# The last stage of a hybrid mixing layer: gated products summed in PSUM, operand casts moved to ScalarE, the residual gate folded into the output weights

## The chip, the cores and the metric

The kernel runs on one core of a Trainium2 chip. The metric is the device time of one execution in microseconds (us), taken as the median of several runs; lower is better. The engines are PE (TensorE, the matrix unit), DVE (VectorE), ACT (ScalarE), POOL (GpSimd) and SP (SyncE, which here only issues transfers). Each engine works through its own list of instructions strictly in order; semaphores make one engine wait for another. SBUF is the working memory, PSUM the small memory (eight banks of 128 x 512 fp32) that PE writes its products to.

## The reference

One layer over 2048 positions of width 1024: a normalised and modulated input is projected, three branches (short convolution `a`, Fourier mixing `f`, neighbourhood attention `c`) give one 2048 x 512 array each, and then, in the part that matters here:

```
y_a = (...) @ w_br_a;  y_f = (...) @ w_br_f;  y_c = (...) @ w_br_c       # each 512 -> 1024
m   = sig(g_a)*y_a + sig(g_f)*y_f + sig(g_c)*y_c                         # 1024 wide
x   = x + gt_l * (m @ w_out)                                             # residual gate gt_l: one number per output column
return rmsnorm(x, final_g)
```

## The kernel before, in words

All matrix work is fp32 in three passes: each operand is split into a high part (a cast to the fp32r type) and a low part (operand minus high part), and `mm3` (lines 125 to 128) issues high x high, high x low, low x high into one PSUM bank. `split` (line 130) does the cast on one engine (line 131) and the subtraction on another (line 132).

The kernel first computes projections, attention and the Fourier part; the order of instructions on each engine is set by the scheduler of the framework, from the program's order, its dependencies and the buffers that it may use. The last stage (lines 1206 to 1273) starts while the last pair of projections is still being computed. It works on four blocks of 512 positions. For each block:

- **Branch operands** (`make_y`, line 1151). For each of the three branches and four pieces k: load the piece (`yr`, two buffers) and its partner, multiply them (line 1177, DVE), cast the product to `yh` and subtract to get `yl`, both on DVE (line 1181). The pieces of the first block are made during the last pair of projections; those of a later block are made while the output products of the block before it run.
- **Branch products** (lines 1228 to 1247). For each of eight output pieces j and three branches: load the weights (`load_wb`: cast `wbh` on ACT, subtraction `wbl` on POOL, three buffers each), load the stored gate `th` (it holds tanh(g/2), so that sig(g) is half of `th` + 1), 12 matmuls into a bank `mm` from `bank()`, which rotates through three banks. DVE then computes (`th` + 1) x bank into SBUF (line 1238) and adds the branches there (line 1240). The sum `acc` is split into `mh` (ACT) and `ml` (DVE). A matmul group of the next output piece needs a free bank: line 1238 of three groups earlier.
- **Output weights** (`load_wo`, line 1212), in the first block only: eight loads of 128 x 1024 through two buffers (`wor`), split into `woh` (ACT) and `wol` (DVE), then kept.
- **Output products** (lines 1248 to 1273). For four tiles of 128 positions and two halves x: 24 matmuls into a bank `po` (two banks), DVE multiplies the bank by the gate `gtb` (line 1261), POOL adds the residual `xr` (line 1262; DVE in the very last tile), ACT squares it and sums along the row (line 1263), then two tiny DVE operations and a POOL power (lines 1264 to 1266) give the row's scale, DVE applies it together with `fg` (line 1269), and SP stores the tile. The buffer `xr` is free for its next load once ACT has squared.

POOL's list holds the 24 `wbl` subtractions of a block, then the eight adds and four powers of its output products, then the 24 of the next block.

Of the kernel before, what the change touches and what calls it, by code (L numbers as in the profile page):

```python
# [11 lines left out]
F32 = mybir.dt.float32  # L12
F32R = mybir.dt.float32r
AF = mybir.ActivationFunctionType
ALU = mybir.AluOpType
# [44 lines left out]
def emit(tc, I, out, dbg=None):  # L60
    nc = tc.nc
# [22 lines left out]
    vtt = nc.vector.tensor_tensor  # L84
    ptt = nc.gpsimd.tensor_tensor
    stt = nc.vector.scalar_tensor_tensor
# [38 lines left out]
    def mm3(ps, ah, al, bh, bl, first, last):  # L125
        nc.tensor.matmul(ps, ah, bh, start=first, stop=False)  # L126
        nc.tensor.matmul(ps, ah, bl, start=False, stop=False)  # L127
        nc.tensor.matmul(ps, al, bh, start=False, stop=last)  # L128

    def split(hi, lo, src, heng, leng):  # L130
        heng.copy(hi, src) if heng is nc.scalar else heng.tensor_copy(hi, src)  # L131
        return leng.tensor_tensor(lo, src, hi.bitcast(F32), ALU.subtract)  # L132
# [27 lines left out]
    def then(a, b):  # L160

        tc.add_manual_dep(b.ins, a.ins.name, mybir.DependencyInfo(mybir.DependencyClass.NoSync, mybir.DependencyReason.DATA), reason="order")
# [151 lines left out]
    def bank():  # L314
        return pm.tile([128, 512], F32, tag="mm", name="mm")
# [827 lines left out]
    c2, pc, wcv, gtb = (C[x] for x in ("c2", "pc", "wcv", "gtb"))  # L1143

    def htile(o, hl, k, name):
        return hpool.tile([128, 512], F32R, tag=f"{o}{hl}{k}", name=name)
# [4 lines left out]
    def make_y(b, br, behind=None):  # L1151
        bs = slice(b * 512, b * 512 + 512)
        for k in range(4):
            yr = c2.tile([128, 512], F32, tag="yr", name="yr")
            load(yr, {"a": sad, "f": sfd, "c": scd}[br][k][b])
            o = c2.tile([128, 512], F32, tag="yo", name="yo")
            if br == "a":
                u = c2.tile([128, 514], F32, tag="u", name="u")
                lo, hi = max(b * 512 - 1, 0), min(b * 512 + 513, S)
                if b == 0:  # L1160
                    nc.vector.memset(u[:, 0:1], 0.0)
                if b == NB - 1:
                    nc.vector.memset(u[:, 513:514], 0.0)
                load(u[:, lo - b * 512 + 1 : hi - b * 512 + 1], ud[k][:, lo:hi])
                nc.scalar.activation(o, u[:, 0:512], AF.Identity, bias=wcv[:, k, 3:4], scale=wcv[:, k, 0:1])
                i = stt(o, u[:, 1:513], wcv[:, k, 1:2], o, ALU.mult, ALU.add)
                if behind:
                    then(behind, i)
                stt(o, u[:, 2:514], wcv[:, k, 2:3], o, ALU.mult, ALU.add)
            elif br == "f":  # L1170
                load(o, fd[k][:, bs])
            else:
                u = c2.tile([128, 514], F32, tag="u", name="u")
                load(u[:, :512], od[k][:, b].rearrange("p a b -> p (a b)"))
                nc.scalar.copy(o.rearrange("p (r ct c) -> p ct r c", r=8, ct=4)[:, :, ::-1, :],
                               u[:, :512].rearrange("p (ct r c) -> p ct r c", ct=4, r=8))
            i = vtt(yr, yr, o, ALU.mult)  # L1177
            if behind:
                then(behind, i)
            a, l = htile(YT[br], "h", k, "yh"), htile(YT[br], "l", k, "yl")  # L1180
            split(a, l, yr, nc.vector, nc.vector)
            yh[br, k], yl[br, k] = a, l

    def load_wb(j, n_):
        wr = c2.tile([128, 512], F32, tag="wr", name="wr", bufs=WRB)
        nc.sync.dma_start(wr, I["w_br"][j, n_])
        wh = c2.tile([128, 512], F32R, tag="wbh", name="wbh", bufs=3)
        wl = c2.tile([128, 512], F32R, tag="wbl", name="wbl", bufs=3)
        split(wh, wl, wr, nc.scalar, nc.gpsimd)
        return wh, wl  # L1190
# [4 lines left out]
    def hook():  # L1195
        br = next(first_y, None)
        if br:
            make_y(0, br)
            wb0.append(load_wb(0, len(wb0)))
# [12 lines left out]
    def load_wo(k):  # L1212
        wr = c1.tile([128, D], F32, tag="xn", name="wor", bufs=2)
        nc.sync.dma_start(wr, I["w_out"][:, k])
        for x in range(2):
            if k < 4:
                woh[k][x], wol[k][x] = (htile(("B22", "T4")[x], hl, k, "wo") for hl in "hl")
            else:
                woh[k][x], wol[k][x] = (c1.tile([128, 512], F32R, tag=f"wo{hl}{k}{x}", name="wo") for hl in "hl")
            split(woh[k][x], wol[k][x], wr[:, x * 512 : x * 512 + 512], nc.scalar, nc.vector)  # L1220

    for b in range(NB):
        bs = slice(b * 512, b * 512 + 512)
        if b:
            for br in "afc":
                make_y(b, br, done)
        mh, ml = [], []
        for j in range(8):
            acc = None
            for n_, br in enumerate("afc"):  # L1230
                wh, wl = wb0.pop(0) if wb0 else load_wb(j, n_)
                th = c2.tile([128, 512], F32, tag="tg", name="tg", bufs=4)
                nc.sync.dma_start(th, gd[n_ * 8 + j][b])
                ps = bank()
                for k in range(4):
                    s = slice(k * 128, k * 128 + 128)
                    mm3(ps, wh[:, s], wl[:, s], yh[br, k], yl[br, k], k == 0, k == 3)
                nc.vector.scalar_tensor_tensor(th, th, 1.0, ps, ALU.add, ALU.mult)  # L1238
                if acc is not None:
                    nc.vector.tensor_tensor(th, th, acc, ALU.add)  # L1240
                acc = th
            for k in (((0, 1),) + tuple((k,) for k in range(2, 8)) + ((),))[j] if b == 0 else ():
                load_wo(k)
            a, l = htile(("T1", "T3")[j // 4], "h", j % 4, "mh"), htile(("T1", "T3")[j // 4], "l", j % 4, "ml")
            done = split(a, l, acc, nc.scalar, nc.vector)
            mh.append(a)
            ml.append(l)
        for t in range(4):
            ts_ = slice(t * 128, t * 128 + 128)
            row = b * 512 + t * 128  # L1250
            end = row == S - 128
            xn = c1.tile([128, D], F32, tag="xn", name="xn", bufs=2)
            sm = c2.tile([128, 4], F32, tag="smc", name="smc")
            for x in range(2):
                cs = slice(x * 512, x * 512 + 512)
                xr = c2.tile([128, 512], F32, tag="xr", name="xr")
                load(xr, I["x"][row : row + 128, cs])
                ps = pc.tile([128, 512], F32, tag="po", name="po")
                for k in range(8):
                    mm3(ps, mh[k][:, ts_], ml[k][:, ts_], woh[k][x], wol[k][x], k == 0, k == 7)  # L1260
                vtt(xn[:, cs], ps, gtb[:, cs], ALU.mult)  # L1261
                (vtt if end else ptt)(xn[:, cs], xn[:, cs], xr, ALU.add)  # L1262
                nc.scalar.activation(xr, xn[:, cs], AF.Square, accum_out=sm[:, x : x + 1])
            nc.vector.tensor_tensor(sm[:, 2:3], sm[:, 0:1], sm[:, 1:2], ALU.add)
            nc.vector.tensor_scalar(sm[:, 2:3], sm[:, 2:3], 1.0 / D, 1e-6, ALU.mult, ALU.add)
            nc.gpsimd.tensor_tensor(sm[:, 3:4], sm[:, 2:3], mhalf[:, 0:1], ALU.pow)
            for x in range(2):
                cs = slice(x * 512, x * 512 + 512)
                nc.vector.scalar_tensor_tensor(xn[:, cs], xn[:, cs], sm[:, 3:4], fg[:, cs], ALU.mult, ALU.mult)  # L1269
                if end:  # L1270
                    (nc.sync, nc.scalar)[x].dma_start(out[row:, cs], xn[:, cs])
            if not end:
                store(out[row : row + 128, :], xn)
# [92 lines left out]
```

## Time and profile before

| | |
|---|---|
| runs (three) | median 2257.54 us, 2255.1 to 2263.36 |
| profiled execution, its own time | 2256.13 us |
| its span in the trace | 2254.4 us |
| busy in the span | PE 2132.9 us (95%), DVE 1547.0 (69%), ACT 887.1 (39%), POOL 1011.5 (45%) |
| last stage | first branch matmul 1766.69, last output matmul ends about 2246.4 |

The span is what the trace covers; the device time is 1.7 us longer. PE is busy nearly all the time, so what can be gained is the time in which PE waits, or runs at a lower clock after it waited. Two traps: matmuls are pipelined, so that a matmul's own duration (0.39 us) is longer than the 0.23 us at which they follow one another; and an engine's busy share says nothing on whether PE waits for it. The useful views are those that show, for one stretch, how long PE was not busy and which instruction ended that.

### The profile page before, as it was taken

How to read it: one execution, taken by the hardware profiler on the slowest of the kernel's cores; microseconds unless marked ns; L12 is line 12 of the kernel's file. 1: busy time of each engine (PE TensorE's matmuls, PEld its weight loads, DVE VectorE, ACT ScalarE, POOL GpSimd, SP SyncE). 2: the span in 40 equal slices, each digit the busy share in tenths (PEclk: the TensorE clock that was granted, in tenths of full speed). 3: DMA queues.
4: the chain of work that ended last, by engine and by line, in shares of the span. 5: the costliest groups of instructions: out<-in, count | busy, mean ns of one | idle time of the engine just before them, and what ended most of it. 6: DMA issues, size and time to landing. Idle time of an engine off the chain costs nothing. (4 is left out here: it accounts for less than half of the span.)

```text
span 2254.4 us, 32033 instructions
## 1 busy us (share of the span) xinstructions
PE 2132.9 (95%) x10588; PEld 1686.6 (75%) x10588; DVE 1547.0 (69%) x2731; ACT 887.1 (39%) x2011; POOL 1011.5 (45%) x761
## 2 busy tenths in 40 slices
PE   6899989999999899999999999999999898999998
PEld 4678768888788687777777777777757677878777
DVE  6864685565665665778787788786736868787773
ACT  3443222334544442454555555554213332222121
POOL 2753467654464654444444334343415243434341
PEclk8999999999999899999999999999999999999999
DMA  6244644233233344343444444453466676666561
GB/s 255 80 136 117 225 174 168 94 108 117 94 101 111 101 142 131 109 126 107 142 127 127 139 148 127 141 149 127 154 211 218 212 223 214 192 206 191 173 190 67
DMA packets 198863, 336.78 MB, mean 149 GB/s; under 512 B 22249, under 2 KB 89129, under 8 KB 197546
## 3 DMA queue, kind: packets, MB, share of 16 engines
q1 hardware_dynamic: 198554, 334.47, 46.8%
q8 instruction: 84, 1.38, 0.3%
q14 instruction: 81, 0.66, 0.1%
q10 hardware_dynamic: 144, 0.26, 0.0%
HBM read 248.27 MB, written 86.38 MB: 148 GB/s over the span
## 5 line engine op out<-in xcount | busy, mean ns | idle before, releaser
L131 ACT CAST wh<-wr 128x512 fp32r<-128x512 f32 x384 | 237.7, 620 | 479.1 <-PE mm L311 388.1
L132 DVE TENSOR_TENSOR wl<-wr,wh 128x512 fp32r<-128x512 f32 x256 | 244.7, 957 | 37.0 <-ACT wh L131 36.8
L132 POOL TENSOR_TENSOR wl<-wr,wh 128x512 fp32r<-128x512 f32 x128 | 173.7, 1360 | 212.8 <-ACT wh L131 191.0
L337 POOL TENSOR_TENSOR ws<-wr 128x512 f32<-128x512 f32 x62 | 89.0, 1435 | 309.0 <-DMA wr<-w_in 255.3
L395 DVE SCALAR_TENSOR_TENSOR st<-mm,bin,tp 128x512 f32<-128x512 f32 x158 | 118.0, 747 | 143.0 <-PE mm L312 136.0
L132 POOL TENSOR_TENSOR wbl<-wr,wbh 128x512 fp32r<-128x512 f32 x96 | 130.9, 1367 | 163.0 <-ACT wbh L131 160.4
L126 PE MATMUL mm<-yh,wbh 128*128 128x512 f32 x384 | 153.5, 400 | 17.8 <-DVE tg L1238 10.4
L128 PE MATMUL mm<-yh,wbl 128*128 128x512 f32 x384 | 152.8, 398 | 2.3 <-POOL wbl L132 2.3
L127 PE MATMUL mm<-yl,wbh 128*128 128x512 f32 x384 | 151.8, 396 | 0.3 <-DVE yl L132 0.3
L931 PE MATMUL tr<-ident,P 128*128 128x128 f32 (+3 forms) x672 | 120.4, 280 | 19.1 <-DVE PT L941 7.9
L132 POOL TENSOR_TENSOR wl<-ws,wh 128x512 fp32r<-128x512 f32 x62 | 83.7, 1350 | 112.5 <-ACT wh L131 94.8
L931 PEld LDWEIGHTS tr<-ident,P 128*128 128x128 f32 (+3 forms) x672 | 78.9, 139 | 68.4 <-DVE PT L941 25.4
L355 POOL TENSOR_TENSOR wr<-wr 128x512 f32<-128x512 f32 x64 | 87.9, 1373 | 93.7 <-DVE wl L132 58.8
L450 DVE TENSOR_TENSOR st<-mm,tp 128x512 f32<-128x512 f32 x96 | 65.9, 686 | 87.2 <-PE mm L312 84.4
L310 PE MATMUL mm<-B11h,wh 128*128 128x512 f32 x256 | 104.5, 408 | 14.0 <-DVE tp L353 7.4
L131 ACT CAST wbh<-wr 128x512 fp32r<-128x512 f32 x96 | 59.2, 620 | 127.6 <-PE mm L127 61.0
L126 PE MATMUL po<-wo,mh 128*128 128x512 f32 x256 | 101.2, 395 | 7.8 <-DVE xn L1261 7.7
L310 PE MATMUL mm<-T4h,wh 128*128 128x512 f32 x256 | 103.1, 403 | 4.5 <-DVE tp L345 4.5
L311 PE MATMUL mm<-B11l,wh 128*128 128x512 f32 x256 | 103.0, 402 | 4.2 <-DVE B11l L132 4.2
L339 POOL TENSOR_TENSOR wr<-ws,wr 128x512 f32<-128x512 f32 x62 | 84.3, 1360 | 49.6 <-DVE wl L132 36.3
L310 PE MATMUL mm<-B21h,wh 128*128 128x512 f32 x256 | 102.6, 401 | 3.6 <-DVE st L450 2.8
L310 PE MATMUL mm<-T2h,wh 128*128 128x512 f32 x256 | 102.8, 402 | 1.4 <-ACT T2h L131 1.4
(319 smaller groups left out, 6293.3 us busy)
## 6 DMA issues: line engine op xcount, KB each, us to landing
wr<-w_in SPq DMA_DIRECT2D x136, 512.0 KB
gd<-st SPq DMA_DIRECT2D x96, 256.0 KB
wr<-w_br SPq DMA_DIRECT2D x96, 256.0 KB
tg<-gd SPq DMA_DIRECT2D x96, 256.0 KB
tab<-dft SPq DMA_DIRECT2D x40, 256.0 KB
wa<-w_ada SPq DMA_DIRECT2D x32, 256.0 KB
rawq<-qd SPq DMA_DIRECT2D x64, 128.0 KB
rawk<-kd SPq DMA_DIRECT2D x64, 128.0 KB
```

The costliest lines, as they stand in the source:

```text
L126: nc.tensor.matmul(ps, ah, bh, start=first, stop=False)
L127: nc.tensor.matmul(ps, ah, bl, start=False, stop=False)
L128: nc.tensor.matmul(ps, al, bh, start=False, stop=last)
L131: heng.copy(hi, src) if heng is nc.scalar else heng.tensor_copy(hi, src)
L132: return leng.tensor_tensor(lo, src, hi.bitcast(F32), ALU.subtract)
L310: nc.tensor.matmul(ps, w[0][:, s], oh, start=first and k == 0, stop=False)
L311: nc.tensor.matmul(ps, w[0][:, s], ol, start=False, stop=False)
L337: ptt(t1, a21, a22, ALU.add)
L339: ptt(a11, t1, a11, ALU.subtract)
L355: ptt(a12, a12, a11, ALU.subtract)
L395: stt(dst, ps, bc(m), add, ALU.add, ALU.add)
L931: nc.tensor.transpose(pt[:w_, x * 128 : x * 128 + 128], src, ident)
```

## The change

Five edits, all in the last stage.

1. The cast to `yh` moves from DVE to ACT (48 casts in all; the subtraction `yl` stays on DVE and so now waits for ACT).
2. Branch products go in turn to a bank of `bank()` (three) and of a new set `pb` (three): six banks in place of three.
3. The gated product of the second and third branch is written back to its own PSUM bank and added from there: into the SBUF tile for the second, into the PSUM bank for the third. `split` then reads the sum from PSUM.
4. `load_wo` multiplies the loaded 128 x 1024 output weights by the gate (one DVE operation per load, eight in all) ahead of the split.
5. The output products are no longer multiplied by the gate; one DVE operation adds the residual to the bank. POOL's add is gone.

```diff
-            split(a, l, yr, nc.vector, nc.vector)
+            split(a, l, yr, nc.scalar, nc.vector)
...
         nc.sync.dma_start(wr, I["w_out"][:, k])
+        vtt(wr, wr, gtb, ALU.mult)
...
+    turn_ = iter(range(1 << 20))
+
+    def branch_bank():
+        return pc.tile([128, 512], F32, tag="pb", name="pb", bufs=3) if next(turn_) % 2 else bank()
...
-                ps = bank()
+                ps = branch_bank()
...
-                nc.vector.scalar_tensor_tensor(th, th, 1.0, ps, ALU.add, ALU.mult)
-                if acc is not None:
-                    nc.vector.tensor_tensor(th, th, acc, ALU.add)
-                acc = th
+                if acc is None:
+                    stt(th, th, 1.0, ps, ALU.add, ALU.mult)
+                    acc = th
+                else:
+                    stt(ps, th, 1.0, ps, ALU.add, ALU.mult)
+                    vtt(acc if n_ == 1 else ps, ps, acc, ALU.add)
...
-            done = split(a, l, acc, nc.scalar, nc.vector)
+            done = split(a, l, ps, nc.scalar, nc.vector)
...
-                vtt(xn[:, cs], ps, gtb[:, cs], ALU.mult)
-                (vtt if end else ptt)(xn[:, cs], xn[:, cs], xr, ALU.add)
+                vtt(xn[:, cs], ps, xr, ALU.add)
```

The line numbers of the changed kernel are seven higher behind `load_wo`: the add of product and residual is its line 1269, the two scalings its 1276, the gate multiplication of the weights its 1215, the two gating operations its 1245 and 1248, the branch add its 1249.

DVE's list in the output products of the first block, between the third and the fourth bank of output products, before (line 1261 empties a bank):

```order
L1261 TENSOR_TENSOR xn<-po,gtb 128x512
L1177 TENSOR_TENSOR yr<-yr,yo 128x512
L131 CAST yh<-yr 128x512
L132 TENSOR_TENSOR yl<-yr,yh 128x512
L1177 TENSOR_TENSOR yr<-yr,yo 128x512
L131 CAST yh<-yr 128x512
L132 TENSOR_TENSOR yl<-yr,yh 128x512
L1261 TENSOR_TENSOR xn<-po,gtb 128x512
```

The same place of the changed kernel (its line 1269 empties a bank):

```order
L1269 TENSOR_TENSOR xn<-po,xr 128x512
L1177 TENSOR_TENSOR yr<-yr,yo 128x512
L132 TENSOR_TENSOR yl<-yr,yh 128x512
L1177 TENSOR_TENSOR yr<-yr,yo 128x512
L132 TENSOR_TENSOR yl<-yr,yh 128x512
L1269 TENSOR_TENSOR xn<-po,xr 128x512
```

The two casts are gone from DVE's list; the multiplication (line 1177) that waits for a load still stands ahead of the next emptying.

DVE's list at the start of the stage, from the emptying of j = 0's second product on, before (the rows for `yr` and `yo` make the operands of branch `c`; the first line 1238 empties j = 0's second product, the next one j = 1's first):

```order
L1238 SCALAR_TENSOR_TENSOR tg<-tg,mm 128x512
L132 TENSOR_TENSOR yl<-yr,yh 128x512
L1240 TENSOR_TENSOR tg<-tg 128x512
L1238 SCALAR_TENSOR_TENSOR tg<-tg,mm 128x512
L1177 TENSOR_TENSOR yr<-yr,yo 128x512 x2
L131 CAST yh<-yr 128x512 x2
L132 TENSOR_TENSOR yl<-yr,yh 128x512 x2
L132 TENSOR_TENSOR wo<-wor,wo 128x512 x2
```

The same place of the changed kernel, down to the first gate multiplications of output weights:

```order
L1248 SCALAR_TENSOR_TENSOR pb<-tg,pb 128x512
L132 TENSOR_TENSOR yl<-yr,yh 128x512
L1249 TENSOR_TENSOR tg<-pb,tg 128x512
L1177 TENSOR_TENSOR yr<-yr,yo 128x512 x2
L132 TENSOR_TENSOR yl<-yr,yh 128x512
L1245 SCALAR_TENSOR_TENSOR tg<-tg,pb 128x512
L132 TENSOR_TENSOR yl<-yr,yh 128x512
L1248 SCALAR_TENSOR_TENSOR mm<-tg,mm 128x512
L1215 TENSOR_TENSOR wor<-wor,gtb 128x1024
L1249 TENSOR_TENSOR mm<-mm,tg 128x512
L1215 TENSOR_TENSOR wor<-wor,gtb 128x1024
```

The last two multiplications of branch `c` (line 1177, x2) stood behind the emptying of j = 1's first product; they now stand ahead of it, and two multiplications of 1024 columns follow.

PE's list in the first block, where the third output piece j = 2 begins (`mm_17659` is the last product of j = 1, `mm_17696` the first of j = 2), before:

```order
L126 MATMUL mm_17659<-yh_17431,wbh_17653 128x512
L127 MATMUL mm_17659<-yl_17432,wbh_17653 128x512
L128 MATMUL mm_17659<-yh_17431,wbl_17654 128x512
L126 MATMUL mm_17696<-yh_17254,wbh_17690 128x512
L127 MATMUL mm_17696<-yl_17255,wbh_17690 128x512
```

The same place of the changed kernel (`pb_17661` and `mm_17699` are those products, `po_18182` and `po_18211` the first two banks of output products, `wo_17585` and `wo_17589` the first output weights, `mh_17604` the first sum):

```order
L126 MATMUL pb_17661<-yh_17431,wbh_17655 128x512
L127 MATMUL pb_17661<-yl_17432,wbh_17655 128x512
L128 MATMUL pb_17661<-yh_17431,wbl_17656 128x512
L126 MATMUL po_18182<-wo_17585,mh_17604 128x512
L126 MATMUL po_18211<-wo_17589,mh_17604 128x512
L126 MATMUL mm_17699<-yh_17254,wbh_17693 128x512
L127 MATMUL mm_17699<-yl_17255,wbh_17693 128x512
```

Two matmuls of the output products now stand ahead of j = 2; before, the first of them stood behind all three branches of j = 2.

## Rows read from the trace of the kernel before

**Rows 1.** Windows of PE: us, busy (matmuls), granted clock, DMA share, GB/s.

```profile
1766.60:1806.20 39.60, 31.12 (x116) 0.91 0.75 245
1806.20:1849.10 42.90, 42.22 (x178) 1.00 0.73 226
1849.10:1894.70 45.60, 43.33 (x188) 1.00 0.69 222
1894.70:1912.00 17.30, 12.91 (x50) 0.90 0.56 179
...
1966.20:2013.00 46.80, 44.47 (x193) 1.00 0.66 210
2013.00:2028.40 15.40, 12.97 (x50) 0.89 0.59 192
2028.40:2082.60 54.20, 54.20 (x240) 1.00 0.61 191
2082.60:2132.60 50.00, 46.09 (x193) 0.97 0.57 185
2132.60:2148.50 15.90, 12.79 (x50) 0.89 0.45 150
```

**Rows 2.** Waits of PE, last stage: total us, times, longest.

```profile
PE mm L126 <- DVE tg L1238: 10.4, 4, 4.4
PE po L126 <- DVE xn L1261: 7.7, 7, 3.6
```

**Rows 3.** Timeline, end of block 0: start, us, what [idle before <- releaser].

```profile
1899.30 0.68 DVE L1261 TENSOR_TENSOR xn<-po,gtb 128x512 f32<-128x512 f32 x1
...
1900.06 1.29 POOL L1262 TENSOR_TENSOR xn<-xn,xr 128x512 f32<-128x512 f32 x1 [1.69 <-DVE xn L1261]
...
1902.14 0.16 DVE L1264 TENSOR_TENSOR smc<-smc 128x1 f32<-128x1 f32 x1 [2.15 <-ACT xr L1263]
...
1903.24 3.41 DVE L1269 SCALAR_TENSOR_TENSOR xn<-xn,smc,fg 128x512 f32<-128x512 f32 x2 [0.76 <-POOL smc L1266]
...
1907.40 0.47 PE L126 MATMUL mm<-yh,wbh 128*128 128x512 f32 x1 [4.39 <-DVE tg L1238]
```

**Rows 4.** Window of PE behind that wait, columns as above.

```profile
1908.00:1912.00 4.00, 4.00 (x12) 0.57 0.81 228
```

**Rows 5.** Timeline, output products of block 2: POOL, SP, DVE.

```profile
2104.72 5.39 POOL L1262 TENSOR_TENSOR xn<-xn,xr 128x512 f32<-128x512 f32 x2 [4.12 <-DVE xn L1261]
...
2109.65 0.33 SPq L1257 DMA_DIRECT2D xr<-x  x1
2110.07 0.86 SPq L1155 DMA_DIRECT2D yr<-sfd  x2
...
2113.36 0.69 DVE L1177 TENSOR_TENSOR yr<-yr,yo 128x512 f32<-128x512 f32 x1 [5.04 <-DMA yr<-sfd]
```

**Rows 6.** Timeline of DVE at the start of the stage.

```profile
1770.23 0.76 DVE L131 CAST yh<-yr 128x512 fp32r<-128x512 f32 x2
...
1783.92 0.69 DVE L1238 SCALAR_TENSOR_TENSOR tg<-tg,mm 128x512 f32<-128x512 f32 x1 [2.61 <-PE mm L128]
```

**Rows 7.** Groups by line and shape, last stage: busy, mean ns, idle before.

```profile
L132 POOL TENSOR_TENSOR wbl<-wr,wbh 128x512 fp32r<-128x512 f32 x93 | 125.8, 1356 | 162.9 <-ACT wbh L131 160.4 <-PE mm L127 2.5
...
L1240 DVE TENSOR_TENSOR tg<-tg 128x512 f32<-128x512 f32 x64 | 82.1, 1282 | 2.0
...
L131 DVE CAST yh<-yr 128x512 fp32r<-128x512 f32 x48 | 29.5, 622 | 0.7
...
L131 ACT CAST mh<-tg 128x512 fp32r<-128x512 f32 x32 | 19.8, 620 | 49.8 <-DVE tg L1240 49.7
```

**Rows 8.** Groups of DVE, whole kernel: two SBUF inputs, 1023 wide.

```profile
L1020 DVE TENSOR_TENSOR ueo<-fu 128x1023 f32<-128x1023 f32 x4 | 5.8, 1444 | 3.0 <-DMA fu<-fud 3.0
...
L1023 DVE TENSOR_TENSOR ueo<-fu 128x1023 f32<-128x1023 f32 x4 | 4.9, 1218 | 0.0
```

**Rows 9.** Timeline of DVE, last tile.

```profile
2247.17 0.69 DVE L1262 TENSOR_TENSOR xn<-xn,xr 128x512 f32<-128x512 f32 x1
```

## The prediction

> **What bounds the kernel now.** I read the windows of PE first. Where nothing waits, PE starts 240 matmuls in 54.2 us, 0.226 us each; three branch stretches run at that pace, one of them shown [rows 1]. Each other window's length less its matmuls at 0.226 is what it lost, idle time and slow clock together: 39.6 - 116 x 0.226 = 13.4 us at the start, 2.7 in the rest of block 0; 3.1, 3.2 and 6.4 in the output products of blocks 0, 1 and 2; 6.0, 4.1 and 4.6 at the three block ends [rows 1]. That is 43.5 us. The reader should see here how small the prize is: with all of it gone the kernel would still take about 2214.
>
> The waits of PE name the cause, DVE: for a free branch bank (line 1238, 10.4 us in 4 waits) and for an emptied output bank (line 1261, 7.7 us in 7) [rows 2]. What DVE was doing is read from the timelines. At the end of block 0, DVE empties the last output bank, POOL adds the residual for 1.29 us, ACT squares, DVE has meanwhile waited 2.15 us, then takes 3.41 us for two scalings, and only behind those stands the line 1238 that frees a bank; PE had used its three banks and waited 4.39 us [rows 3]. Then it ran at 0.57 of full clock, that is mostly at 1.2 in place of 2.4 GHz: 12 matmuls in 4.0 us in place of 2.7 [rows 4]. So a wait is paid about 1.3 us more than it lasts.
>
> In the output products of block 2 the order of events is: POOL's two adds stretch to 5.39 us; SP, which issues in order, sends the next `xr` load only after ACT's square of that sum, 2109.65, and the `yr` loads queued behind it at 2110.07; DVE waits 5.04 us for that `yr`, until 2113.36, with the emptying of an output bank behind it in its list [rows 5].
>
> **Part by part.** The sum is against the profiled execution: span 2254.4, device time 2256.13; the median of the runs is 1.4 above that.
>
> *Six banks, and POOL's add gone, at the block ends.* PE can now start six groups ahead of DVE instead of three. Three groups last 36 x 0.226 = 8.1 us, the wait was 4.39 at its longest [rows 2, 3]. What is late next is the weights: the fourth group's `wbl` stands on POOL behind the power of the last tile, and POOL needs 1.36 per group against 2.7 of PE [rows 7]. The power comes at least 1.29 us earlier, since the add ahead of it is gone [rows 3]. Loss 14.7 before; I leave 0.7, so -14.0. Bounds: -14.7 when the weights are never late, -7 when they take half of the place of the banks.
>
> *Output products.* DVE loses 12 casts per block, 12 x 0.62 = 7.4 us [rows 7], in 193 x 0.226 = 43.6 us of PE's work. POOL's add leaves both chains of rows 5: the square follows DVE's sum directly, so `xr` is free and SP moves on sooner by the add's 1.29 us [rows 3], or by 4.1 where it is stretched (5.39 less one add of 1.29). Two banks give each emptying 24 x 0.226 = 5.4 us before PE notices. New is that `yl` waits for ACT's cast; ACT's list has the squares and the copies for the next branches among these casts, and behind a late square a cast is late; behind the waiting `yl` stand the next multiplication and the next emptying of a bank, for which PE waits. One cast on ACT is 0.62 [rows 7]. Loss 12.7 before; I leave 3.2, one late bank per block, so -9.5. Bounds: -12.7, and +5 if all 36 casts lengthen the way from load to release (0.62 less 0.38, plus two hand-offs of 0.08 as between 1899.98 and 1900.06 in rows 3, is 0.40 each, 14 us, of which I let PE see a third).
>
> A cast on DVE takes 0.38 where nothing disturbs it (two in 0.76) [rows 6], and 0.62 on the mean [rows 7]. The Trainium skill, "VectorE: DVE Perf Modes", section "Mode 2×_2P", gives the reason for the short one: a copy of fp32 within SBUF uses both read ports and makes two results per cycle. By that rule the move makes every cast slower by 0.24, since ScalarE's is 0.62; the trace agrees for single casts and not for the mean. Going by the rule alone the output products would gain about 5 us less.
>
> *Start of the stage.* Two effects of opposite sign. The operands of the first block come pair by pair: two multiplications, two casts, two subtractions, then the buffers are free and the next loads go out. With the casts on ACT beside the second multiplication the first buffer comes free some 0.6 us sooner, three pairs ahead of branch `c`: 2 us. Line 1238 of the next j, for which DVE waited 2.61 us at 1783.92 with `c`'s last pair behind it [rows 6], now stands behind that pair: 1.7 us. Together -3.7. Against it: eight multiplications of 1.22 to 1.44 us, taken from the nearest operation (two SBUF inputs, 1023 wide) [rows 8]: 9.8 to 11.6 us on DVE, each waiting for its load with the gating and adding of branch products queued behind it; six banks let PE go on. DVE gets as much back in these 65 us: its 16 branch adds took 1.28 with both inputs in SBUF and should take 0.68 like line 1261, which has one in PSUM [rows 3, 7]: 16 x 0.6 = 9.6. But the first two matmuls of the output products stand ahead of j = 2, and need one such multiplication, a cast of the weights and a cast of `mh` on ACT, and the next weights' cast stands behind those on ACT. PE gets there 17 x 0.226 = 3.8 us after the last product of j = 0. Behind that product come its gating 0.68, a multiplication 1.33, two casts of weights 1.24 and the cast of `mh` 0.62, 3.9 us and some hand-offs; then the next `wbh` 0.62 and `wbl` 1.36, at 6 us or later, where PE would want that `wbl` at about 4.3: 2 us. So -1.7. Bounds: -6 (no delay from the weights), +8 (each of the eight multiplications delays PE by 1.2 beyond the cover).
>
> Those eight have a rule against them. The operands of POOL's `wbl` and of these multiplications lie in SBUF, and rows 5 show POOL at 5.39 us for two adds while DVE worked. The Trainium skill, "SBUF — State Buffer", section "Who interferes with whom", says that a VectorE instruction with two SBUF inputs and a GpSimd instruction that reads SBUF exclude each other for a whole instruction. By that each multiplication could hold back one `wbl` by its full 1.22 to 1.44, about 10 us in block 0, and the start would cost 6 more than I sum. The adds in PSUM give back as many exclusions by the same rule.
>
> *Writing to PSUM.* No DVE operation of the kernel before writes PSUM. Reading from it costs 0.68 (line 1261 [rows 3]); I take that, and as the upper end 1.28 [rows 7]. Even this would add 0.6 x 24 = 14 us to a block's 65 us of branch products, in which DVE follows a PE that it does not delay in three windows. No cost on the path; below nothing is excluded there because PE is the bound.
>
> *End.* In the last tile DVE did both operations; one of 0.69 us goes [rows 9], and nothing covers it: -0.7.
>
> Sum: -14.0 - 9.5 - 1.7 - 0.7 = -25.9: 2256.1 - 25.9 = 2230.2 for a profiled execution, about 2232 as a median.
>
> **Rivals.**
>
> A, the loads stay. DVE freed of casts only waits longer for the same `yr`. A load takes 3.3 us from issue to use (2110.07 to 2113.36 [rows 5]); from use to release there are a multiplication 0.69, a cast 0.62 and a subtraction like the first, 2.0 us [rows 5, 7]; with two buffers twelve loads take 12 x 5.3 / 2 = 32 us of the 43.6, and every stall of SP adds. For it: DVE's longest wait was for this load. Against it: that wait began with POOL's add. Then the output products gain nothing, and the start loses its 1.7: 2232 + 11 = 2243.
>
> B, the bank wait becomes a weights wait: at each block end the `wbl` of the fourth group comes late, with the slow clock behind it. For it: POOL's list is unchanged there. Against: 1.36 against 2.7 per group. Block ends gain 7, output products 5: 2257.5 - 7 - 5 - 0.7 = 2245.
>
> C, slower: the output weights in block 0. Each of the later `wor` loads waits for DVE to be done with its buffer, and on SP the loads of branch weights, which PE needs within 2.7 us, are queued behind it. If each of the eight holds these up by a multiplication and a load, 1.33 + 3.3 = 4.6, that is 37 us, and the rest of the sum (-24) does not cover it: 2257.5 + 13 = 2270. It decides once the hold-up passes 3 us per load. For it: the DMA share in block 0 is the highest (0.75 and 0.73 [rows 1]). Against: three groups of weights are buffered.
>
> **How the numbers follow.** Forecast 0.63, A 0.17, B 0.10, C 0.07, and 0.03 for no effect at all. 0.5%, about what can be told from no change, is 11.3 us: faster means below 2246. The forecast (its own range 2223 to 2240), A, and a little over half of B are faster: 0.63 x 0.98 + 0.17 x 0.75 + 0.06 = 0.81. C is slower: 0.06. The rest, 0.13, is the same. The range: at its low end the terms' best bounds, -14.7 - 12.7 - 6 - 0.7 = -34, 2223; I go to 2221. At its high end it takes in A and B, 2248.
>
> **What would show it.** Right: windows of PE at the three block ends without waits for line 1245 or 1248 and at full clock; waits for the emptying of output banks (line 1269 there) down from 7.7 to about 2; DVE's branch adds near 0.68; POOL with no add between the `wbl`. Wrong: waits of PE on `wbl` or `wbh` of several us at the block ends (B), DVE waits for `yr` of about 5 us with banks emptied late behind them (A), a window of block 0 that loses clearly more than 16 us with PE waiting on `wo` or weights (C), or operations that write PSUM at well over 0.7.

## The result, and the profile after

The changed kernel takes 2223.8 us where the kernel before takes 2258.2 in the same set of runs: a ratio of 0.985, with an interval of 0.982 to 0.988. Measured a second time it came to 2225.4 against 2253.5, 0.988 (0.985 to 0.990). The forecast was 2232, the range 2221 to 2248.

Its profiled execution was the longest of its four: 2231.0, span 2229.2. The last stage begins there with the branch matmul at 1769.95; before it was 1766.7. In the fourteen profiles of this case that moment lies between 1762.9 and 1770.8, so 4 us either way come from ahead of the stage. The stage itself is therefore compared by its own windows. This is the view that answers to [rows 1], cut at the first matmul of each stretch (a branch stretch has 288 matmuls, an output stretch 192; the count also takes in one that reaches over the edge, and some of block 0's output matmuls lie in its branch stretch):

```profile
1769.95:1849.99 80.04, 72.65 (x295) 0.96 0.74 247
1849.99:1891.94 41.95, 41.95 (x186) 1.00 0.73 231
1891.94:1960.69 68.75, 66.47 (x289) 1.00 0.64 202
1960.69:2004.21 43.52, 43.52 (x193) 1.00 0.72 233
2004.21:2069.49 65.28, 65.28 (x289) 1.00 0.65 199
```

From 1960 on, to the end of the stage at 2221.8, PE has no gap and full clock: 65.28 us for 288 matmuls and 43.52 for 192, 0.2267 each. Cut in the same way, the trace before has 82.4 and 45.6 for block 0, then 71.6, 46.8, 69.6, 50.0, 70.1 and 43.5.

What a stretch lost is its length less 0.2267 for each of its matmuls. For all profiles, in us; "ends" are the branch stretches of blocks 1 to 3 (their loss lies in the first groups, where a block ends), "products" the output stretches of the four blocks:

| kernel | block 0 | ends 1, 2, 3 | products | stage | time: ratio to before |
|---|---|---|---|---|---|
| before | 15.8 | 6.3, 4.3, 4.8 | 13.2 | 44.4 | 1 |
| changed, first / second profile | 13.2 / 13.6 | 3.5, 0, 0 / 3.0, 0, 0 | 0.0 / 2.0 | 16.7 / 18.6 | 0.985 / 0.988 |
| less six banks | 16.0 | 4.2, 0, 0 | 1.4 | 21.6 | 0.990 |
| less casts on ScalarE | 17.0 | 4.5, 0, 0 | 0.0 | 21.4 | 0.989 |
| less products in PSUM | 14.6 | 2.3, 0, 3.3 | 2.9 | 23.2 | 0.990 |
| less gate in weights | 9.6 | 4.4, 2.0, 2.1 | 5.0 | 23.0 | 0.991 |
| before, plus six banks | 16.2 | 2.5, 0.5, 0.9 | 11.4 | 31.6 | 0.995 |
| before, plus casts on ScalarE | 11.9 | 3.6, 6.2, 5.3 | 9.0 | 36.0 | 0.996 |
| before, plus gate in weights | 18.8 | 6.5, 0, 4.2 | 0.0 | 29.6 | 0.994 |

The stage lost 44.4 and now loses 16.7 to 18.6, so it is shorter by 25.8 to 27.7; another 0.8 goes behind the last output matmul (2254.4 - 2246.2 = 8.2 before, 2229.2 - 2221.8 = 7.4 after). The two ratios, 28 and 34 us, hold the same gain and the chance of what lies ahead of the stage. Each kernel of the table has one profile, the changed kernel two; these two differ by 1.9 in the stage's loss, so a difference of 2 us in that column alone shows nothing.

The waits of PE in the last stage (total, times, longest) answer to [rows 2]. Neither the branch bank (10.4 before) nor the output bank (7.7) is in the list any more (the second profile has one wait of 0.8 us for an output bank). What is left is the start and the weights:

```profile
PE mm L126 <- ACT yh L131: 3.3, 1, 3.3
PE pb L126 <- ACT wbh L131: 2.3, 2, 1.4
PE pb L128 <- POOL wbl L132: 2.0, 4, 0.6
PE mm L128 <- POOL wbl L132: 1.6, 2, 1.1
```

The groups that answer to [rows 7] and [rows 8]: the add of the branches fell from 1282 to 698 ns though it writes PSUM, the gating there takes 693, the cast on ACT 619, and one of the eight multiplications 1364:

```profile
L1248 DVE SCALAR_TENSOR_TENSOR mm<-tg,mm 128x512 f32<-128x512 f32 x32 | 22.2, 693 | 38.2 <-PE mm L128 38.2
L1249 DVE TENSOR_TENSOR mm<-mm,tg 128x512 f32<-128x512 f32 x16 | 11.2, 698 | 0.5
L131 ACT CAST yh<-yr 128x512 fp32r<-128x512 f32 x48 | 29.7, 619 | 72.0 <-DVE yr L1177 70.8 <-DVE u L1163 1.2
L1215 DVE TENSOR_TENSOR wor<-wor,gtb 128x1024 f32<-128x1024 f32 x8 | 10.9, 1364 | 0.0
```

**The 3.5 us left at the first block end.** Timelines of DVE, POOL, SP and PE there; this answers to [rows 3]:

```profile
1895.12 0.69 DVE L1177 TENSOR_TENSOR yr<-yr,yo 128x512 f32<-128x512 f32 x1 [1.61 <-DMA yr<-scd]
1897.16 0.69 DVE L1269 TENSOR_TENSOR xn<-po,xr 128x512 f32<-128x512 f32 x1
1899.74 3.46 DVE L1276 SCALAR_TENSOR_TENSOR xn<-xn,smc,fg 128x512 f32<-128x512 f32 x2 [0.76 <-POOL smc L1273]
```

```profile
1899.67 2.98 POOL L132 TENSOR_TENSOR wbl<-wr,wbh 128x512 fp32r<-128x512 f32 x2
```

```profile
1903.23 0.34 SPq L1280 DMA_DIRECT2D out<-xn  x1
1903.66 0.38 SPq L1186 DMA_DIRECT2D wr<-w_br  x1
```

```profile
1907.64 0.50 PE L126 MATMUL pb<-yh,wbh 128*128 128x512 f32 x1 [1.35 <-ACT wbh L131]
```

Read it as a chain: a late `yr` load holds DVE 1.61 us, with the last emptying of an output bank behind it. ACT's square of that tile (1897.88) waits for this, and behind it in ACT's list stand the casts of two `wbh` (1898.51), so their `wbl` come on POOL only at 1899.67, behind the tile's power. PE waits 0.27 us at 1901.01 for the first of them, that of the fourth group. The two scalings then meet these two `wbl` and take 3.46; the store of the tile waits for them, and on SP the next load of branch weights stands right behind the store. One of the two buffers for this load came free when the first `wbl` ended, at 1900.96; the load goes out at 1903.66, 11.7 us after the block's first matmul, so the store may have held it up by 2.7 us. PE reaches its sixth group 5 x 12 x 0.2267 = 13.6 us after that first matmul, had nothing delayed it, and finds no `wbh`; most of the 3.5 us goes there. At the next block end DVE waits for no load between the emptyings of the last two banks, the scalings take 2.45 beside one `wbl`, and the load goes out at 2009.98, 5.8 us after that block's first matmul:

```profile
2009.98 0.38 SPq L1186 DMA_DIRECT2D wr<-w_br  x1
```

### The profile page after: what moved, and what is told of

The parts are those of the page before. It is cut to its first block, busy times and chain, and to the rows that moved or that the text cites. A ratio compares the mean times of both kernels' runs of the same rounds, so it can differ in the third digit from the quotient of the medians.

```text
span 2229.2 us, 31997 instructions
## 1 busy us (share of the span) xinstructions
PE 2125.4 (95%) x10588; PEld 1684.4 (76%) x10588; DVE 1479.1 (66%) x2689; ACT 913.1 (41%) x2059; POOL 956.2 (43%) x731
## 5 line engine op out<-in xcount | busy, mean ns | idle before, releaser
L931 PE MATMUL tr<-ident,P 128*128 128x128 f32 (+3 forms) x672 | 120.0, 280 | 17.8 <-DVE PT L941 8.9
L941 ACT COPY PT<-tr 128x128 f32<-128x128 f32 (+2 forms) x240 | 57.4, 286 | 118.1 <-PE tr L931 118.0
L310 PE MATMUL mm<-B22h,wh 128*128 128x512 f32 x256 | 103.2, 403 | 1.6 <-DVE tp L341 1.6
L312 PE MATMUL mm<-T4h,wl 128*128 128x512 f32 x256 | 102.5, 400 | 1.0 <-DVE wl L132 1.0
L312 PE MATMUL mm<-B11h,wl 128*128 128x512 f32 x256 | 102.9, 402 | 0.5 <-DVE wl L132 0.4
```

The source lines that it names most:

```text
L310: nc.tensor.matmul(ps, w[0][:, s], oh, start=first and k == 0, stop=False)
L312: nc.tensor.matmul(ps, w[1][:, s], oh, start=False, stop=last and k == 3)
L931: nc.tensor.transpose(pt[:w_, x * 128 : x * 128 + 128], src, ident)
```

## The experiments

First four parts undone (edits 4 and 5 belong together) one at a time in the changed kernel, then three of them made alone in the kernel before, with the changed kernel once more; last, three tries at what is left, and all three together. A ratio is to the kernel before on the same chip.

**Three banks again.**

```diff
-                ps = branch_bank()
+                ps = bank()
```

> The changed kernel with its branch products on three banks again in place of six; all else stays. Theory 1, as the prediction's sum has it (the banks, with the add gone from POOL, are what removed the waits at the block ends): PE waits for a branch bank (lines 1245, 1248) at all three block ends again, 10 us or more with the slow clock behind them, and the time is 2234 or more. Theory 2 (DVE is earlier at the block ends by itself, and the banks are mostly spare): in the changed kernel's trace the fourth group of blocks 2 and 3 starts at 2012.4 and 2121.2, and the gating that would free its bank of three ends at 2010.1 and 2119.0, so no wait there; only in block 1 is the group (1900.1) ahead of that gating (1903.8). Then one block end waits 3.7 us, partly in place of the 1.5 us for weights that is there already, and the time is 2224 to 2229.

Measured: 2231.7 us, 0.990 (0.988 to 0.992). Blocks 2 and 3 lose nothing with three banks, so theory 2 holds for the ends (blocks 0 and 2 here):

```profile
1762.87:1845.08 82.21, 73.02 (x292) 0.94 0.75 241
2002.04:2067.32 65.28, 65.28 (x289) 1.00 0.65 201
```

The time is above what theory 2 gave, and where it went neither theory had: block 0, 16.0 in place of 13.2 to 13.6. PE's longest wait is there, for `ml`. Since the sum of the branches now stays in its bank, that bank is free only after DVE's `ml`, and `ml` stood behind four subtractions of output weights:

```profile
PE mm L126 <- DVE ml L132: 3.5, 1, 3.5
```

```profile
1786.58 4.63 DVE L132 TENSOR_TENSOR wo<-wor,wo 128x512 fp32r<-128x512 f32 x4
1791.14 0.68 DVE L132 TENSOR_TENSOR ml<-mm,mh 128x512 fp32r<-128x512 f32 x1
```

So with the other parts in, the extra banks serve block 0 (about 2.6 us) more than the block ends.

**Casts on DVE again.**

```diff
-            split(a, l, yr, nc.scalar, nc.vector)
+            split(a, l, yr, nc.vector, nc.vector)
```

> The changed kernel with the cast of the branch operands (yh) on DVE again; all else stays. Theory 1 (these casts held up the emptying of output banks): 12 x 0.62 = 7.4 us of DVE come back in each block's output products, which lose about 3 us each again with PE waiting for line 1269; 2230 to 2234. Theory 2 (the casts were not what PE waited for; the gate's multiplication and POOL's add were): the output products stay without waits, the start changes by 2 us at most either way, 2222 to 2226.

Measured: 2229.6 us, 0.989 (0.988 to 0.991). The output products stay without a gap, as theory 2 has it; that the start changes by 2 us at most is wrong, block 0 loses 17.0 in place of 13.2 to 13.6:

```profile
1765.51:1850.01 84.50, 75.30 (x298) 0.94 0.72 232
```

A cast on DVE took 446 ns on the mean here, and 622 before the change [rows 7]:

```profile
L131 DVE CAST yh<-yr 128x512 fp32r<-128x512 f32 x42 | 18.5, 446 | 0.5
```

**Products in SBUF again.**

```diff
-                if acc is None:
-                    stt(th, th, 1.0, ps, ALU.add, ALU.mult)
-                    acc = th
-                else:
-                    stt(ps, th, 1.0, ps, ALU.add, ALU.mult)
-                    vtt(acc if n_ == 1 else ps, ps, acc, ALU.add)
+                nc.vector.scalar_tensor_tensor(th, th, 1.0, ps, ALU.add, ALU.mult)
+                if acc is not None:
+                    nc.vector.tensor_tensor(th, th, acc, ALU.add)
+                acc = th
...
-            done = split(a, l, ps, nc.scalar, nc.vector)
+            done = split(a, l, acc, nc.scalar, nc.vector)
```

> The changed kernel with the gated products and their sum in SBUF again, as before the change; six banks, casts and gate stay. Theory 1 (no cost on the path, as the prediction has it): the adds take 1.28 again in place of 0.69, 64 x 0.59 = 38 us more of DVE, and PE waits no longer than now: 2222 to 2227. Theory 2 (the adds with two SBUF inputs and POOL's subtractions hold each other up, and the multiplications of the output weights need the DVE time that the short adds give back): block 0 loses 5 to 10 us more, with PE waiting for wbl or a bank, 2229 to 2234.

Measured: 2231.9 us, 0.990 (0.989 to 0.992), against both theories in part: the time is that of theory 2, the place is not. The adds cost 1113 ns again and PE waits for `wbl` more often, but block 0 loses only 1 more:

```profile
L1246 DVE TENSOR_TENSOR tg<-tg 128x512 f32<-128x512 f32 x64 | 71.2, 1113 | 2.0
```

```profile
PE pb L128 <- POOL wbl L132: 3.9, 5, 1.1
PE mm L128 <- POOL wbl L132: 2.6, 3, 1.1
```

3.3 us of the stage's extra 5 are the chain of the first block end at the third: scalings of 3.46 us (2117.59), and the weights' load issued behind the store 12.0 us after the block's first matmul. Whether the adds in SBUF put it there, or it comes and goes between executions, one profile doesn't tell.

```profile
2109.54:2178.15 68.61, 66.15 (x289) 1.00 0.54 170
```

```profile
2121.51 1.15 SPq L1186 DMA_DIRECT2D wr<-w_br  x2
```

**Gate back at the output products.**

```diff
         nc.sync.dma_start(wr, I["w_out"][:, k])
-        vtt(wr, wr, gtb, ALU.mult)
...
-                vtt(xn[:, cs], ps, xr, ALU.add)
+                vtt(xn[:, cs], ps, gtb[:, cs], ALU.mult)
+                (vtt if end else ptt)(xn[:, cs], xn[:, cs], xr, ALU.add)
```

> The changed kernel with the residual gate applied to the output products again (DVE multiplies the bank by the gate, POOL adds the residual, DVE in the last tile) and no multiplication of the output weights; banks, casts and PSUM products stay. Theory 1 (the add on POOL and the longer chain to the release of xr were what delayed the output products): they lose 6 to 9 us again in three blocks with PE waiting for output banks, and block 0 gains 2 to 3 since eight multiplications are gone: 2228 to 2233 with 0.7 at the end. Theory 2 (the casts on ACT relieve DVE enough): no waits in the output products, and block 0 gains 2 to 4: 2219 to 2223.

Measured: 2232.4 us, 0.991 (0.989 to 0.992); theory 1 in kind, with sizes off. Block 0 gains 3.6 to 4.0 (the price of the eight multiplications), the output products lose 5.0 (6 to 9 were expected) with PE waiting for their banks, and every block end loses 2 or more:

```profile
1764.01:1840.91 76.90, 71.79 (x297) 0.98 0.79 257
1953.12:1998.70 45.58, 44.15 (x193) 1.00 0.68 211
1998.70:2065.99 67.29, 66.42 (x289) 1.00 0.62 200
```

```profile
PE po L126 <- DVE xn L1268: 3.3, 5, 0.8
```

**The changed kernel again**, beside the three single edits.

> The changed kernel itself once more, as the measure for the three single edits beside it and for the four undone edits before. By its ratio of 0.985 it takes 2220 where the kernel before takes 2254; its last stage should lose about 18 us to waits and slow clock, as in the first profile. If the single undone edits cost what their medians say (2230 to 2232), it must stay below 2226; if those medians differ from it by chance alone, it comes out near 2230.

Measured: 2225.4 us, 0.988 (0.985 to 0.990), stage loss 18.6. It is just below the 2226 that the first case needs, and the stage loses what was expected. But its interval overlaps those of all four undone edits: the windows, not the times, carry the verdicts on single parts.

**Six banks alone.** The kernel before with `ps = branch_bank()`, nothing else.

> The kernel before with six branch banks and nothing else. Theory 1 (banks alone free the block ends): the 16.2 us that the branch products of blocks 1 to 3 lose fall to 5 or less, the output products stay at 13.7: ratio about 0.995. Theory 2 (the wait moves to the weights, rival B): PE goes on until the fourth group and waits there for wbl, which stands behind the last power on POOL and the last add before it; the block ends lose 9 or more, ratio 0.997 or above.

Measured: 2243.2 us, 0.995 (0.994 to 0.997). Theory 1: the three ends fall from 15.4 to 4.0, the output products stay at 11.4 (by another cut the expectation has 16.2 and 13.7 for the 15.4 and 13.2 of the table). What is left at the ends is in part theory 2's: PE's waits for `wbl` add up to 2.4 us, and at all three ends the load of weights goes out as soon as a `wbl` on POOL has freed its buffer, 7.9 to 10.0 us after the block's first matmul. Block 1:

```profile
1890.56:1958.35 67.79, 66.08 (x289) 1.00 0.64 201
1958.35:2005.26 46.91, 44.75 (x193) 1.00 0.68 212
```

**Casts on ScalarE alone.** The kernel before with the one line of `split` changed.

> The kernel before with the cast of the branch operands on ScalarE and nothing else. Theory 1 (DVE's 7.4 us of casts per block are what held up the emptying): the output products fall from 13.7 lost to 5 or less, the block ends by 2 or 3 since DVE reaches the last emptying earlier: ratio 0.994 to 0.995. Theory 2 (POOL's add and the loads behind it set the pace): the output products still lose 10 or more, ratio 0.998 or above.

Measured: 2244.9 us, 0.996 (0.995 to 0.998). Neither theory: the output products still lose 9.0, close to theory 2, and the sum of the ends does not move, but block 0 falls by 3.9, and that is nearly half of the gain of 8.4; the output products give 4.2.

```profile
1763.54:1841.68 78.14, 71.60 (x292) 0.98 0.78 253
2002.36:2073.84 71.48, 68.17 (x289) 0.95 0.61 188
```

**Gate in the output weights alone.** The kernel before with the multiplication in `load_wo` and one DVE add for each output bank.

> The kernel before with the residual gate in the output weights (eight multiplications in block 0, one DVE operation in place of DVE and POOL at each output bank) and nothing else. Theory 1 (POOL's add was the cause in the output products, and part of it at the block ends): output products from 13.7 to 4 or less, block ends from 16.2 to 11 or less, block 0 loses up to 3 more: ratio 0.992 to 0.994. Theory 2 (the eight multiplications cost what the rest gives, rival C): with three banks and adds in SBUF block 0 loses 10 more, ratio 0.998 or above.

Measured: 2238.0 us, 0.994 (0.992 to 0.996), theory 1. The output products lose nothing at all, with the casts still on DVE; the second block end loses nothing with three banks; block 0 pays 3.0:

```profile
1764.03:1850.81 86.78, 75.67 (x300) 0.92 0.71 228
1850.81:1891.66 40.85, 40.85 (x181) 1.00 0.75 234
2006.99:2072.27 65.28, 65.28 (x289) 1.00 0.63 200
```

**Late store.** The changed kernel; the store of a block's last tile is written later in the program.

```diff
-            if not end:
+            if t == 3 and not end:
+                held.append((row, xn))
+            elif not end:
                 store(out[row : row + 128, :], xn)
...
+            if j == 0 and held:
+                r_, x_ = held.pop()
+                store(out[r_ : r_ + 128, :], x_)
```

> The changed kernel with the store of each block's last tile (not of the very last) written behind the first three weight loads of the next block; all else stays. What is left of the block ends in the changed kernel is 3.3 to 3.7 us at the first, none at the others. Theory 1 (SP issues in order: the store waits for the scaling of the last tile, and the weight loads for the fourth group stand behind it): block 1 loses 1.5 or less, the PE wait for wbh there goes, and the time falls by about 2, which the time alone can't tell. Theory 2 (POOL's list or DVE's late scaling itself holds the weights): block 1 still loses 3 or more.

Measured: 2224.4 us, 0.986 (0.984 to 0.988); block 1 lost 1.9. This did not test what it was made for: the scheduler put the store ahead of the weights' load on SP all the same:

```profile
1896.95 0.34 SPq L1253 DMA_DIRECT2D out<-xn  x1
1897.38 0.38 SPq L1186 DMA_DIRECT2D wr<-w_br  x1
```

Only the moment differs, 10.4 us after the block's first matmul (1886.94). In the runs with the gate in the weights, six banks and the products in PSUM, the loss goes with that moment: 5.8 us, nothing (block 2 above); 8.6, 0.1 (one load to each j, below); 10.4, 1.9; 11.7, 3.5; 12.1, 4.5 (casts on DVE). That fits the chain; it is no proof of it, since the store was never taken out of the way, and the store is not all of it: with the products in SBUF the first block end lost 2.3 us although its load went out at 9.9, as soon as a `wbl` had freed the buffer.

**Three buffers for `yr`.**

```diff
-            yr = c2.tile([128, 512], F32, tag="yr", name="yr")
+            yr = c2.tile([128, 512], F32, tag="yr", name="yr", bufs=3)
```

> The changed kernel with three buffers for the loaded branch operands (yr) in place of two; all else stays. PE's longest wait left is 3.0 to 3.3 us at 1776, for the cast of branch c's first operand, whose load was late. Theory 1 (the load waits for a buffer): that wait goes, block 0 loses 9 to 11 in place of 13.4 to 13.8. Theory 2 (the loads of the first block are held by what the DMA engines move there, 0.75 busy before the change, or by their order on SP): block 0 loses 13 or more, or the loss moves to the next branch.

Measured: 2223.4 us, 0.986 (0.984 to 0.988). PE's wait of 3.3 us for branch `c` is gone, as theory 1 has it, and block 0 loses 11.3 (9 to 11 were expected). But part of the loss moves, as theory 2 allows: PE now waits at j = 2, 1.8 us for an output weight (1790.78) and 1.7 for a `wbh` (1793.00); block 0's output products lose 1.8, with one wait of 1.5 for an output bank; and the wait for DVE just ahead of the stage is 2.8, where the changed kernel had 1.0 and 1.6. The first block end loses nothing any more. There DVE waits for no `yr` ahead of the last emptying, and the scalings take 2.45:

```profile
1892.62:1957.90 65.28, 65.28 (x289) 1.00 0.61 190
```

```profile
PE mm L126 <- DVE tp L353: 2.8, 1, 2.8
PE po L126 <- ACT wo L131: 1.8, 1, 1.8
PE po L126 <- DVE xn L1269: 1.5, 1, 1.5
```

```profile
1895.48 2.45 DVE L1276 SCALAR_TENSOR_TENSOR xn<-xn,smc,fg 128x512 f32<-128x512 f32 x2 [0.76 <-POOL smc L1273]
```

**One load of output weights to each j.**

```diff
-            for k in (((0, 1),) + tuple((k,) for k in range(2, 8)) + ((),))[j] if b == 0 else ():
+            for k in ((j,)) if b == 0 else ():
```

> The changed kernel with the eight loads of output weights spread one to each output piece j of block 0, in place of two at the first, one at each of the next six and none at the last. Theory 1 (the doubled load, its two multiplications and its four casts and subtractions crowd out the first weights of branches): block 0 loses 11 or 12 in place of 13.4 to 13.8, the output products of block 0 at most 1 more. Theory 2 (what crowds them out is each single load on SP and each pair of casts on ACT, not the double): block 0 loses 13 or more, and the last weights come late for the output products, 2 or more there.

Measured: 2221.1 us, 0.985 (0.983 to 0.987). Block 0 lost 11.8 and its output products 0.3, as theory 1 has it; the first block end lost 0.1. The stage loses 12.2.

**All three, and three buffers for `wr`.** The three edits above with `WRB = 3`.

> The changed kernel with all three together and a third buffer for the loaded branch weights: late store, three yr, one load of output weights to each j, three wr. If the three theories 1 hold and add up, block 0 loses 7 to 9, block 1 at most 1.5, and the time is 6 to 8 below the changed kernel's 2223: 2215 to 2217, ratio to the kernel before 0.983 to 0.985. If the start is set by what the DMA engines must move, block 0 stays at 12 or more and the time within 2 of the changed kernel's.

Measured: 2222.5 us, 0.986 (0.984 to 0.988). The stage loses only 9.7, the least of all, and all of it in block 0: more than the 7 to 9 of the first case, less than the 12 of the second. PE's wait for branch `c` is gone, and its longest is now one of 3.5 us for a `wbh` (1791.77). The wait of 2.8 ahead of the stage, 1.0 and 1.6 in the changed kernel, takes 1.2 to 1.8 of the gain back, and the 2215 to 2217 of the first case was missed. The time is not below that of the changed kernel by more than the interval: whatever the four tries took from the stage, 1 to 9 us, is of the size of what the part ahead of it varies by. None of the four is shown to be faster than the changed kernel.

## Why the prediction was right, by its own steps

**The bound.** What the windows lost, 43.5 by the prediction's cuts, was the whole prize, and no run went below the floor of 2214. With 16.7 of the loss left in the first profile, PE has no gap from the output products of block 1 on.

**Block ends, -14.0.** Measured -11.9 (15.4 to 3.5) and -12.4. The step gave the banks and POOL's add as one cause. The runs part them: the banks alone take 11.4 of the 15.4, the gate's edit, which removes POOL's add and leaves DVE one operation for each bank as before, 4.6 (15.4 to 10.8), nearly all at the second end; with everything else in, blocks 2 and 3 need no more than three banks. At the second end the banks alone leave 0.5 and the gate's edit alone nothing, so the two do not add up; at the third the gate's edit alone is not enough, 4.2 stay. What is late next is the weights, as the step said, and POOL's list has a part in it as it said: the fourth group's `wbl` stands behind the power, for 0.27 us of waiting. The larger part, the sixth group's late load, the step did not have: by the rows above the load was behind the store on SP. The 0.7 left for the weights was too little, 3.0 to 3.5 came.

**Output products, -9.5.** Measured -13.2 and -11.2, the better bound of the step or near it. This is the term of the sum that was most mis-sized, and the reason given first for it was the lesser one: the casts alone take 4.2 of 13.2, the gate's edit alone all 13.2, and putting the casts back on DVE costs nothing there. The second half of the step was right: POOL's add leaves both chains of [rows 5], the square follows DVE's sum, and the next `xr` load goes out sooner. From the start of a bank's emptying to that load it took 3.2 us before (median of 30), 3.0 with the casts alone, and 1.5 with the gate's edit alone and in the changed kernel, as here in block 1:

```profile
1966.85 0.69 DVE L1269 TENSOR_TENSOR xn<-po,xr 128x512 f32<-128x512 f32 x1
```

```profile
1968.32 0.33 SPq L1265 DMA_DIRECT2D xr<-x  x1
```

DVE's load was not what counted: in the output products of block 1 it was busy 34.20 of 46.52 us with the casts alone, and PE lost 3.0 there; with the gate's edit alone it was busy 35.75 of 43.52, and PE lost nothing. No run takes the add off POOL by itself, without the rest of the gate's edit. The late bank that was kept back for each block did not come in the first profile, and 2.0 us in all in the second. For an output bank of block 2 PE waited in neither.

**Start, -1.7.** Measured -2.6 and -2.2 in block 0. Its two effects were near in size: earlier casts -3.7, measured -3.9 alone and -3.4 to -3.8 by undoing; output weights +2.0, measured +3.0 alone and 3.6 to 4.0 by undoing. The sizes agree better than the reasons. The gain of the casts alone is 2.4 us at the stage's 60th matmul, where the step's two reasons lie (it gave them 3.7), and reaches 3.9 only later in block 0, by waits that it did not name. The `wbl` that it saw 2 us late at j = 2 made PE wait 1.15 (1796.38); the rest of the cost of the multiplications came elsewhere. The difference is made up by banks and PSUM products: undone, they cost block 0 2.4 to 2.8, and 1.0 to 1.4. The banks alone, without the multiplications, gained nothing there (16.2 after 15.8); the PSUM products were not run alone.

**Writing PSUM, no cost.** 0.69 to 0.70 for gating and adding, the value taken (0.68) and not the upper end (1.28). It may be more than free: without it the stage lost 4.6 to 6.5 more, of which 3.3 is the open case above; the 1.3 to 3.2 that stay are little beside the 1.9 by which the two profiles of the changed kernel differ.

**End, -0.7.** Measured -0.8.

**The sum.** -25.9 against -26.6 to -28.5 for the stage and its end. The sum is nearer than its terms, and that is luck: the block ends gave 1.6 to 2.1 less than forecast, the output products 1.7 to 3.7 more. The median, 8 below the forecast, holds besides what the part ahead of the stage varies by. In the profile itself the difference is 25.2, because the stage began 3.3 later there.

**The rivals.** A (the loads stay): a late `yr` is there at the first block end and at the start, and its sign came: DVE waits longer for what line 1177 needs, 17.8 us before, 28.2 in the changed kernel. But its price did not come. With the gate's edit alone, the casts and the two buffers as before, these waits are 24.3 us, the longest 3.2 where it was 5.0, and the output products lost nothing. B (banks become weights): true at one end of three, for 3.5 us. C (block 0 grows): the multiplications cost 3 to 4 us in all, not 4.6 each, with three banks (3.0) as with six; what covered the rest no run shows.

**The two rules weighed.** By the Trainium skill, "SBUF — State Buffer", section "Who interferes with whom", a VectorE instruction with two SBUF inputs and a GpSimd one that reads SBUF keep each other out for a whole instruction. The traces agree in kind: two scalings took 3.46 us beside two `wbl` in the chain above, 2.45 in the run with three `yr`, where POOL was at one, and 1.41 with POOL idle, as this row of the changed kernel has it; but in block 0 it did not cost the 6 us that the prediction worked out from it.

```profile
2000.35 1.41 DVE L1276 SCALAR_TENSOR_TENSOR xn<-xn,smc,fg 128x512 f32<-128x512 f32 x2 [0.75 <-POOL smc L1273]
```

By the Trainium skill, "VectorE: DVE Perf Modes", section "Mode 2×_2P", a copy of fp32 within SBUF makes two results per cycle; by that the casts should have been cheaper on DVE. They were, 446 ns against 619 on ACT, once POOL's add was gone, and nothing came of it in the output products, where PE waited for neither.

## What to carry to other kernels

Where two waits have the same engine behind them, making each edit alone tells which one is worth what: here three edits that gave 13, 8 and 15 us alone gave 26 to 28 with a fourth, since two of them cured the same waits, at a block end and in the output products. When an engine's busy share suggests relief, look first at what its list is waiting for: twelve casts off DVE took 4.2 of the 13.2 us from the output products, the edit that takes one add off POOL took all of it, and the rows point to the add's place, between two engines and ahead of a load. And once the waits are gone, look at the queue that issues the loads: here a store that waited for its data had a load of weights right behind it, 2.7 us after that load's buffer was free.

## What was not expected of the hardware

After the wait of 3.3 us for branch `c`, TensorE ran for about 6 us (1779.6 to 1785.6) at a granted clock of 0.50, that is 1.2 GHz; after the wait of 1.35 us at the first block end it kept 1.00. The windows of PE at both places (the second lies within those 6 us):

```profile
1775.50:1780.00 4.50, 1.16 (x3) 0.88 0.87 292
1780.00:1784.00 4.00, 4.00 (x10) 0.50 0.71 203
1905.00:1910.00 5.00, 3.02 (x12) 1.00 0.89 291
```

So the long wait was paid beyond its length, and the short one was not paid in clock.

The add of two branches in SBUF is no fixed price: 1282 ns before, 1113 with every edit but this one, 933 with six banks alone. In PSUM it was 689 to 698 wherever it was looked at.
